# A hybrid layer with linear attention: stores issued by ScalarE, w_out loaded in steps, the sample unit in fourth place

## The chip, the cores and the metric

The kernel runs on one core of a Trainium2 chip. The core has five engines, each with its own row of instructions that it works off in order: TensorE (PE, matrix products; its weight loads are listed as PEld), VectorE (DVE), ScalarE (ACT), GpSimd (POOL) and SyncE (SP), which here does nothing but issue transfers. Transfers between the chip's memory and the core's buffers are issued by an engine and then run beside it. The metric is the time of one execution on the device, in microseconds.

## The reference

One layer of a recurrent decoder is applied to a prompt of 2048 tokens and to a group of samples (8 sequences of 8 tokens, each with states of its own). The width is 1024.

```
h = x @ w_in                               # split into the parts of two head groups
o_gla = rms_norm(gla(q, k, v, log_a, s_gla)) * silu(gate)           # 4 heads
dq, dk, dv = silu(conv(...))               # causal convolution of width 4, then l2 norm of dq, dk
o_gdn = rms_norm(gdn(dq, dk, dv, g, beta, s_gdn)) * silu(gate)      # 4 heads
x = layer_norm(alpha * x + concat(o_gla, o_gdn) @ w_out)
x = layer_norm(alpha * x + (silu(x @ w_gate) * (x @ w_up)) @ w_down)
```

Both attention forms are computed in chunks. In a chunk of GLA the products within the chunk and the product with the state are added, and the state is decayed and raised by k times v. Gated DeltaNet (GDN) solves a triangular system of each chunk first,

```
a_mat = eye + strict_lower(beta * (k k^T) * gamma)
u, w = solve(a_mat, [v * beta, k * beta * exp(gcum)])
delta = u - w @ S
o = (q * exp(gcum)) @ S + ((q k^T) * gamma) @ delta
S = exp(g_last) * S + (k * exp(g_last - gcum))^T @ delta
```

and the next chunk needs its S. Outputs are the layer's result, the new states of prompt and samples, and the last columns of the convolution.

## The kernel before

The 2112 tokens form 17 units: unit 0 holds the 64 sample tokens, units 1 to 16 hold 128 prompt tokens each. Block 0 is the units 0, 1 and 2, and block b the units 1+2b and 2+2b. The stages follow each other in time:

- phase_in, to about 697 us: the projection with w_in, token tiles of 352, weights split into a high and a low part (ScalarE casts the high part at line 185, VectorE subtracts the low part at line 128). The convolution's results cv go to the chip's memory as dq (line 348, 72 stores), the gates as gt and the other parts as qk and v (line 419).
- load_out and phase_gdn, about 697 to 1036 us. load_quad loads w_out in pieces of 128x1024 through two buffers named wraw, scales a piece on VectorE (line 176), casts it on ScalarE (line 177) and subtracts on VectorE. phase_gdn works through groups of units, [0], [1, 2], [3, 4] and so on. rows(b) makes the decay rows of a block, prepare(u) loads q, k and vf of a unit (line 832) and makes its matrix (y at line 846), inversion(group) solves for all units of the group together in seven levels (a product at line 891, a cast P on ScalarE at line 895, products at 898 and 901, copies on VectorE at 904 and 905), advance(u) takes a unit through the state (S at line 940; its result is copied to on at line 263 and stored at 268), and advance_samples does this for unit 0 with the eight states Sh of the sample. While a group advances, the inversion of the next group is done level by level between its products.
- phase_gla, from 1036 us. proj makes gates, q and k of a block and transposes its v (line 527); mix takes the units of the block through the products within the chunk (line 579 and following) and the state; the sample's own states are applied at lines 668 to 696. Between the blocks project(u) does the product with w_out (lines 252 to 254), the layer norm, and stores the transposed result x1T (line 1129) for the next stage. The last nine units are projected after the last block, to about 1450 us.
- The feed-forward part, to the end.

The kernel is written as one program; a scheduler sets the order of each engine's row, by its own estimate of when operands are ready, and by buffers: a tile can be written only when the earlier user of its buffer is done. The two wraw buffers are shared by the pieces of w_out, the sample's states (Sh in GDN, S in GLA) and the x that project adds. keep (lines 256 to 268) copies a result to on, of which there is one buffer, and stores it. All stores are issued by SyncE (ST). A second copy of the GLA stage and what follows stands behind a flag and isn't executed.

## Time and profile before

| what | value |
|---|---|
| time, median of three runs | 2890.68 us (2885.3 to 2898.66) |
| the profiled execution, its own time | 2893.11 us |
| its span | 2891.3 us |
| TensorE busy | 2692.6 us, 93% |
| VectorE busy | 1961.2 us, 68% |
| ScalarE busy | 1229.6 us, 43% |
| GpSimd busy | 1150.5 us, 40% |

The span is the time from the first to the last instruction in the profile; the execution's own time is 1.8 us longer. A busy share is a mean over all stages. Waits are listed with the one that came last. Idle time of an engine counts only where the work that ends the stage waits for it.

### The profile page before, as it was taken

What the parts mean: (1) busy time and instruction counts of PE and PEld (TensorE: products, weight loads), DVE (VectorE), ACT (ScalarE), POOL (GpSimd) and SP (SyncE); (2) the same over time, 40 slices, a digit from 0 to 9 for tenths busy, and PEclk for the clock granted to TensorE, in tenths of its full rate; (3) what the DMA queues carried; (4) which work ended last, traced back from release to release, by engine and by line L of the source; (5) the groups of instructions that cost most, each with busy time, mean ns of one, the idle gap of its engine ahead of it and who ended that gap; (6) DMA issues with size and microseconds to landing.
All of it is one profiled execution on the core that took longest, in us unless ns stands there. A gap on an engine that the chain in (4) does not pass through costs nothing. (4 is left out here: it accounts for less than half of the span.)

```text
span 2891.3 us, 45834 instructions
## 1 busy us (share of the span) xinstructions
PE 2692.6 (93%) x16390; PEld 2451.7 (85%) x16390; DVE 1961.2 (68%) x3185; ACT 1229.6 (43%) x2671; POOL 1150.5 (40%) x1196
## 2 busy tenths in 40 slices
PE   7999999996888868999799999999999999999996
PEld 6998899896777746777589999999999987887885
DVE  7668668665777635776788779877977753646664
ACT  5536536534444323444334445444544432334442
POOL 5343333232543112333586557755555520201111
PEclk9999999998689968999899999999999999999998
DMA  7245235233543033555673326432432334546652
GB/s 252 98 139 190 87 133 168 99 109 116 155 112 85 27 90 113 173 171 162 182 252 115 112 99 204 153 107 99 151 115 102 106 130 139 195 138 232 220 207 91
DMA packets 253156, 406.79 MB, mean 141 GB/s; under 512 B 28488, under 2 KB 211384, under 8 KB 232056
## 3 DMA queue, kind: packets, MB, share of 16 engines
q1 hardware_dynamic: 252488, 403.35, 42.3%
q8 instruction: 131, 2.15, 0.3%
q14 instruction: 105, 0.86, 0.1%
q10 hardware_dynamic: 432, 0.43, 0.0%
HBM read 305.13 MB, written 98.58 MB: 140 GB/s over the span
## 5 line engine op out<-in xcount | busy, mean ns | idle before, releaser
L128 DVE TENSOR_TENSOR wl<-wr,wh 128x512 fp32r<-128x512 f32 x652 | 597.4, 920 | 342.0 <-ACT wh L185 339.3
L229 PE MATMUL p<-xh,wh 128*128 128x352 f32 x2520 | 815.4, 324 | 8.4 <-DVE t L128 4.4
L230 PE MATMUL p<-xl,wh 128*128 128x352 f32 x2520 | 814.6, 323 | 4.1 <-DVE xl L128 4.1
L231 PE MATMUL p<-xh,wl 128*128 128x352 f32 x2520 | 814.4, 323 | 0.7 <-DVE wl L128 0.7
L185 ACT CAST wh<-wr 128x512 fp32r<-128x512 f32 x652 | 402.4, 621 | 581.1 <-PE p L230 283.5
L229 PEld LDWEIGHTS p<-xh,wh 128*128 128x128 f32 x2520 | 474.6, 188 | 10.3 <-ACT wh L185 4.7
L230 PEld LDWEIGHTS p<-xl,wh 128*128 128x128 f32 x2520 | 474.5, 188 | 5.9 <-DVE xl L128 5.9
L231 PEld LDWEIGHTS p<-xh,wl 128*128 128x128 f32 x2520 | 474.0, 188 | 1.0 <-DVE wl L128 1.0
L128 DVE TENSOR_TENSOR t<-t,p 128x352 f32<-128x352 f32 x630 | 318.8, 518 | 202.2 <-PE p L231 200.7
L131 POOL TENSOR_TENSOR wt<-wr 128x512 f32<-128x512 f32 x180 | 243.4, 1352 | 250.0 <-DVE wl L128 222.4
L185 ACT CAST wh<-wt 128x512 fp32r<-128x512 f32 x270 | 167.8, 622 | 316.3 <-PE p L230 271.3
L1051 POOL TENSOR_SCALAR mv<-mv 128x1 f32<-128x1 f32 (+1 forms) x34 | 21.4, 631 | 548.2 <-DVE mv L1050 548.2
L128 DVE TENSOR_TENSOR wl<-wt,wh 128x512 fp32r<-128x512 f32 x270 | 204.9, 759 | 24.2 <-ACT wh L185 20.8
L1237 PE MATMUL p<-wh,hh 128*128 128x512 f32 x528 | 205.4, 389 | 0.0
L1238 PE MATMUL p<-wl,hh 128*128 128x512 f32 x528 | 205.4, 389 | 0.0
L131 POOL TENSOR_TENSOR wt<-wr,wt 128x512 f32<-128x512 f32 x90 | 119.1, 1324 | 212.5 <-DVE wl L128 212.3
L319 PE MATMUL p<-xh,wh 128*128 128x352 f32 x576 | 189.7, 330 | 12.5 <-ACT xh L185 12.5
L1239 PE MATMUL p<-wh,hl 128*128 128x512 f32 x528 | 201.2, 389 | 0.0
L335 DVE SCALAR_TENSOR_TENSOR cv<-hb,cw,cv 128x352 f32<-128x352 f32 (+1 forms) x216 | 151.7, 705 | 58.3 <-ACT cv L333 50.3
L320 PE MATMUL p<-xl,wh 128*128 128x352 f32 x576 | 189.6, 329 | 0.4 <-DVE xl L128 0.4
L321 PE MATMUL p<-xh,wl 128*128 128x352 f32 x576 | 189.8, 330 | 0.0
L131 POOL TENSOR_TENSOR t<-t 128x352 f32<-128x352 f32 x132 | 159.8, 1212 | 53.3 <-ACT t L93 31.2
(278 smaller groups left out, 4790.7 us busy)
## 6 DMA issues: line engine op xcount, KB each, us to landing
wr<-in_w_gu SPq DMA_DIRECT2D x66, 1024.0 KB
wr<-in_w_dn SPq DMA_DIRECT2D x55, 1024.0 KB
wr<-in_w_p SPq DMA_DIRECT2D x42, 1024.0 KB
hid<-t SPq DMA_DIRECT2D x132, 176.0 KB
xr<-in_xT SPq DMA_DIRECT2D x96, 176.0 KB
dq<-cv SPq DMA_DIRECT2D x72, 176.0 KB
xr<-x1T SPq DMA_DIRECT2D x72, 176.0 KB
hr<-hid SPq DMA_DIRECT2D x66, 192.0 KB
```

What stands on the lines that cost most here:

```text
L128: nc.vector.tensor_tensor(out, a, b, op=op)
L131: nc.gpsimd.tensor_tensor(out, a, b, op=op)
L185: nc.scalar.copy(h[:, :N], raw)
L229: nc.tensor.matmul(ps, lhsT=h[:, ks], rhs=x[k][0], start=k == 0, stop=False)
L230: nc.tensor.matmul(ps, lhsT=h[:, ks], rhs=x[k][1], start=False, stop=False)
L231: nc.tensor.matmul(ps, lhsT=l[:, ks], rhs=x[k][0], start=False, stop=k == 3)
L319: nc.tensor.matmul(ps, lhsT=h(k), rhs=x[k][0], start=n == 0, stop=False)
L320: nc.tensor.matmul(ps, lhsT=h(k), rhs=x[k][1], start=False, stop=False)
L321: nc.tensor.matmul(ps, lhsT=l(k), rhs=x[k][0], start=False, stop=n == 7)
L1237: nc.tensor.matmul(p, lhsT=hh[:, ts], rhs=wd[i][0], start=f == 0, stop=False)
L1238: nc.tensor.matmul(p, lhsT=hh[:, ts], rhs=wd[i][1], start=False, stop=False)
L1239: nc.tensor.matmul(p, lhsT=hl[:, ts], rhs=wd[i][0], start=False, stop=f == NF - 1)
```

## The change

1. Stores of results that ScalarE has written are issued by ScalarE: dq (72), gt (48), on (in keep), and x1T (36). The other stores stay on SyncE.
2. load_quad becomes a generator that yields after each piece of w_out. phase_gdn takes one piece after each group, and what is left at the end.
3. The groups of GDN are [1, 2], [3, 4], [5, 6], [0], [7, 8] and so on, and rows(b) is called up to two groups ahead.
4. In GLA the transposes of v move from proj to mix, mix of unit 0 comes behind block 3, and project takes the units in the order 1 to 5, 0, 6 to 16. For the sample the tile at is cleared on GpSimd first.

```diff
-    def load_quad(pool, tag, src, gain):
+    def load_quad(wh, wl, src, gain):
...
             vtt(wl[:, k:k + 2, :], raw, wh[:, k:k + 2, :].bitcast(F32), TT.subtract)
-        return wh, wl
+            yield
...
         if len(dst.shape) == 4:
             for s in range(2):
-                ST.dma_start(out=dst[:, s], in_=on[:C, 2 * s:2 * s + 2])
+                nc.scalar.dma_start(out=dst[:, s], in_=on[:C, 2 * s:2 * s + 2])
         else:
-            ST.dma_start(out=dst, in_=on[:C])
+            nc.scalar.dma_start(out=dst, in_=on[:C])
...
             act(cv, cv, AF.Silu)
             t0 = FT * ib + FN * i
-            ST.dma_start(out=dq_d[f][:, t0:t0 + FN], in_=cv)
+            nc.scalar.dma_start(out=dq_d[f][:, t0:t0 + FN], in_=cv)
...
-                    ST.dma_start(out=to[c + j][:, t0:t0 + FN], in_=t)
+                    (nc.scalar if to is gt_d else ST).dma_start(out=to[c + j][:, t0:t0 + FN], in_=t)
...
         for b in range(NBLK):
-            mix(b, proj(b))
+            r = proj(b)
+            if b == 0:
+                r0 = r
+            mix([u for u in blocks[b][2] if u], r)
+            if b == 3:
+                mix([0], r0)
             yield
...
-        groups = [[0]] + [[u, u + 1] for u in range(1, NU, 2)]
+        groups = [[u, u + 1] for u in range(1, NU, 2)]
+        groups.insert(3, [0])
+        blk = [us[0] // 2 for us in groups]
...
         rows(0)
         start(0)
+        rows(1)
         for _ in inversion(groups[0]):
             pass
         start(1)
         for n, us in enumerate(groups):
+            if n + 2 < len(groups) and blk[n + 2] > 1:
+                rows(blk[n + 2])
...
             for _ in steps:
                 pass
+            next(more, None)
             start(n + 2)
+        for _ in more:
+            pass
...
+        order = [1, 2, 3, 4, 5, 0] + list(range(6, NU))
...
-                project(b)
+                project(order[b])
```

VectorE's row at the start of the GDN stage, before: wraw is a piece of w_out, o1l the low part of its second half, y and at belong to a unit (64x4x64 is the sample, 128x512 a prompt unit), and wr, lr, grs and rr are decay rows.

```order
L773 SCALAR_TENSOR_TENSOR grs_7833<-misc_61,lr_8030 8x256
L128 TENSOR_TENSOR o1l_7796<-wraw_7797,o1h_7795 128x1024
L775 SCALAR_TENSOR_TENSOR rr_8032<-nr_8031,grs_7833 4x256
L176 TENSOR_SCALAR wraw_7802<-wraw_7802,gain_7771 128x1024
L764 TENSOR_SCALAR wr_8626<-wr_8626,gsc_7826 8x256
L846 SCALAR_TENSOR_TENSOR y_7934<-g_7929,gb_7917 64x4x64
L128 TENSOR_TENSOR at_7948<-g_7943,gb_7917 64x4x64
L176 TENSOR_SCALAR wraw_7807<-wraw_7807,gain_7771 128x1024
```

The same engine at its first y in the changed kernel:

```order
L764 TENSOR_SCALAR wr_7983<-wr_7983,gsc_7786 8x256
L128 TENSOR_TENSOR o0l_7774<-wraw_9544,o0h_7773 128x1024
L426 TENSOR_SCALAR wr_7983<-wr_7983 8x256
L128 TENSOR_TENSOR lr_7984<-wr_7983,ls_7990 8x256
L767 TENSOR_SCALAR lr_7984<-lr_7984,gsc_7786 8x256
L773 SCALAR_TENSOR_TENSOR grs_7793<-misc_61,lr_7984 8x256
L775 SCALAR_TENSOR_TENSOR rr_7986<-nr_7985,grs_7793 4x256
L764 TENSOR_SCALAR wr_8428<-wr_8428,gsc_7786 8x256
L846 SCALAR_TENSOR_TENSOR y_7894<-g_7889,gb_7877 128x512
L128 TENSOR_TENSOR at_7908<-g_7903,gb_7877 128x512
```

The first y is now that of unit 1; of the pieces of w_out only the first three stand ahead of it (the third one's subtraction is the second row here), and the other five stand some 300 rows further down.

ScalarE's row where units 3 and 4 are advanced, before and then changed: P is the cast in the inversion, on the copy of a unit's result, on1 its place in the chip's memory.

```order
L895 CAST P1_7838<-inv_8860 128x64x4
L93 ACTIVATE c_rq_176<-c_r_177,lnq_7831 128x4
L93 ACTIVATE ckh_10222<-ckh_10222 128x4
L263 COPY on_9110<-po_9101 128x512
L93 ACTIVATE eR_10220<-R_10218 128x4x129
L93 ACTIVATE nr_10688<-nr_10688,epsl_69 8x256
L895 CAST P2_7839<-inv_8877 128x32x8
```

```order
L840 COPY vt_9577<-g_9572 128x512
L895 CAST P0_7797<-inv_8966 128x128x2
L262 COPY on_9100<-po_9091 128x512
L895 CAST P1_7798<-inv_8983 128x128x2
L267 DMA on1_3_91<-on_9100 128x512
L93 ACTIVATE eR_10221<-R_10219 128x4x129
L895 CAST P2_7799<-inv_9000 128x64x4
```

In the changed kernel the store (line 267) stands one row behind its copy, or two, and the casts of the next level stand behind the store.

TensorE's row at the sample's place in GLA, before (527 transposes v, 579 and 634 begin a unit, 668, 682 and 690 are the sample's own, 944 and 945 the end of GDN):

```order
L944 MATMUL po<-S,qe 128x128
L945 MATMUL po<-de,at 128x128
L944 MATMUL po<-S,qe 128x128
L945 MATMUL po<-de,at 128x128
L944 MATMUL po<-S,qe 128x128
L945 MATMUL po<-de,at 128x128
L527 MATMUL g<-ident,vf 64x128 x4
L527 MATMUL g<-ident,vf 128x128 x8
L579 MATMUL g<-qz_12297,kn 64x2x64 x2
L634 MATMUL g<-ident,ek 64x128 x2
L668 MATMUL px<-v,at_12303 64x128 x2
L682 MATMUL px<-S_12399,qm 64x128 x4
```

The same place in the changed kernel, where these lines have the numbers 531, 574, 629, 663, 677 and 685, and 647 is the last product of unit 8:

```order
L643 MATMUL g<-S,qz_12298 128x128
L647 MATMUL g<-v,kz 128x128 x4
L531 MATMUL g<-ident,vf 64x128 x4
L574 MATMUL g<-qz_12297,kn 64x2x64 x2
L629 MATMUL g<-ident,ek 64x128 x2
L663 MATMUL px<-v,at_12303 64x128 x2
L677 MATMUL px<-S_13278,qm 64x128 x4
L685 MATMUL g<-v,khm 64x128 x2
L677 MATMUL px<-S_13278,qm 64x128 x4
L685 MATMUL g<-v,khm 64x128 x2
```

The sample's products now stand behind those of unit 8; no product with w_out stands between them.

## Rows read from the trace of the kernel before

**Rows 1.** The page of the profile: the span, TensorE's busy time, and the row of the forty slices (72.3 us each) for TensorE's busy share, in tenths.
```profile
span 2891.3 us, 45834 instructions
...
PE 2692.6 (93%) x16390; PEld 2451.7 (85%) x16390; DVE 1961.2 (68%) x3185; ACT 1229.6 (43%) x2671; POOL 1150.5 (40%) x1196
...
PE   7999999996888868999799999999999999999996
```

**Rows 2.** Busy time by stretches of 20 us, the stretch, its length, then busy us and number of instructions of PE, PEld, DVE, ACT and POOL, the granted clock (1.00 is full), the DMA engines' share and GB/s. The first row lies in the projections, the next five in the GDN stage, the last three at the start of the GLA stage.
```profile
480.00:500.00 20.00, 18.45 (x101) 15.07 (x101) 17.71 (x27) 12.66 (x30) 13.38 (x17) 1.00 0.42 138
700.00:720.00 20.00, 4.67 (x25) 3.15 (x25) 14.26 (x31) 8.95 (x20) 6.87 (x12) 0.50 0.81 215
720.00:740.00 20.00, 10.27 (x50) 9.12 (x51) 18.25 (x27) 14.68 (x39) 15.47 (x24) 0.50 0.57 154
740.00:760.00 20.00, 20.00 (x126) 18.11 (x126) 10.38 (x18) 8.12 (x23) 11.52 (x12) 0.59 0.77 209
...
780.00:800.00 20.00, 16.38 (x147) 14.76 (x146) 17.65 (x36) 6.32 (x21) 7.68 (x10) 0.84 0.70 191
900.00:920.00 20.00, 15.52 (x205) 14.22 (x206) 14.04 (x33) 7.62 (x18) 6.11 (x7) 0.91 0.17 45
1040.00:1060.00 20.00, 9.00 (x46) 6.75 (x46) 7.12 (x24) 5.79 (x15) 5.33 (x12) 0.52 0.76 201
1060.00:1080.00 20.00, 14.95 (x89) 10.69 (x84) 4.29 (x16) 2.79 (x13) 2.67 (x11) 0.50 0.15 44
1080.00:1100.00 20.00, 18.00 (x71) 9.59 (x72) 6.32 (x17) 1.98 (x8) 2.66 (x5) 0.70 0.17 44
```

**Rows 3.** VectorE's timeline in the GDN stage (start, duration, both in us): the cast with which the inversion of a pair begins (line 128, DT from inv), and the update of S (line 940) of the first unit of the pairs (1, 2), (3, 4) and (5, 6), and of unit 16, the last.
```profile
817.62 1.28 DVE L128 TENSOR_TENSOR DT<-inv,half 128x512 f16<-128x512 f32 x2
...
819.81 1.12 DVE L940 SCALAR_TENSOR_TENSOR S<-S,eGl,seq 128x128 f32<-128x128 f32 x4 [0.21 <-PE seq L938]
...
854.39 1.12 DVE L940 SCALAR_TENSOR_TENSOR S<-S,eGl,seq 128x128 f32<-128x128 f32 x4 [0.21 <-PE seq L938]
...
884.81 1.12 DVE L940 SCALAR_TENSOR_TENSOR S<-S,eGl,seq 128x128 f32<-128x128 f32 x4 [0.21 <-PE seq L938]
...
1035.28 1.12 DVE L940 SCALAR_TENSOR_TENSOR S<-S,eGl,seq 128x128 f32<-128x128 f32 x4 [3.14 <-PE seq L938]
```

**Rows 4.** VectorE's timeline at the start of the GDN stage: y (line 846) of the sample (64 rows), of unit 1 and of unit 2 (128 rows each), and the cast that begins the inversion of the pair (1, 2).
```profile
721.36 0.42 DVE L846 SCALAR_TENSOR_TENSOR y<-g,gb 64x256 f32<-64x256 f32 x1
...
736.42 0.69 DVE L846 SCALAR_TENSOR_TENSOR y<-g,gb 128x512 f32<-128x512 f32 x1
...
744.41 0.69 DVE L846 SCALAR_TENSOR_TENSOR y<-g,gb 128x512 f32<-128x512 f32 x1 [0.18 <-PE g L844]
...
765.42 1.27 DVE L128 TENSOR_TENSOR DT<-inv,half 128x512 f16<-128x512 f32 x2
```

**Rows 5.** ScalarE's timeline there: gb, the operand of y, of unit 1.
```profile
723.45 1.28 ACT L93 ACTIVATE gb<-R,c_nb 128x128 f32<-128x128 f32 x4
```

**Rows 6.** Groups of instructions of the GDN stage (690 to 1040 us; line, engine, operation, tiles, shapes and count, then busy us and mean ns of one, then the idle time before them and what ended it): TensorE's four large groups for the sample, whose lines no other unit uses.
```profile
L993 PE MATMUL seq<-de,khm 64*128 64x128 f32 x64 | 13.1, 369 | 0.5 <-DVE Sh L128 0.5
...
L966 PE MATMUL seq<-kq,Sh 128*128 128x16 f32 x64 | 12.6, 344 | 2.6 <-DMA Sh<-in_state_gdn 2.6
...
L982 PE MATMUL po<-ident,fm 128*64 128x128 f32 x8 | 2.8, 448 | 0.0
L983 PE MATMUL po<-de,at 64*64 64x128 f32 x8 | 2.7, 445 | 0.0
```

**Rows 7.** The same view: VectorE's work on the pieces of w_out, eight in all (the scale, and the low part of the second four).
```profile
L176 DVE TENSOR_SCALAR wraw<-wraw,gain 128x1024 f32<-128x1024 f32 x8 | 9.2, 1156 | 5.5 <-DMA wraw<-in_w_out 4.6 <-DMA gain<-in_norm_g 0.9
...
L128 DVE TENSOR_TENSOR o1l<-wraw,o1h 128x1024 fp32r<-128x1024 f32 x4 | 5.1, 1273 | 0.0
```

**Rows 8.** ScalarE's queue at the start of the program: one of the transfers that it issues (start, duration of the issue).
```profile
1.16 0.45 ACTq L304 DMA_DIRECT2D hist<-in_conv  x1
```

**Rows 9.** Waits: who waited at which line for whom, us in all, times, longest. First ScalarE and then TensorE up to 700 us, then TensorE in the GDN stage.
```profile
ACT wh L185 <- PE p L230: 163.7, 146, 1.4
...
PE p L319 <- ACT xh L185: 12.5, 2, 8.3
...
PE inv L898 <- ACT P L895: 24.5, 48, 0.8
```

**Rows 10.** Waits of SyncE's DMA queue over the whole span, the same columns: the stores of on and of x1T.
```profile
SPq L268 <- ACT on L263: 156.9, 14, 22.3
...
SPq L1129 <- ACT x1T L1125: 37.3, 17, 5.2
```

**Rows 11.** TensorE's timeline from the end of the GDN stage: the last product of GDN, the transposes of v (with the wait ahead of them in brackets), the sample's first product, and the first transposes for w_out after the sample's run.
```profile
1036.42 0.39 PE L945 MATMUL po<-de,at 128*128 128x128 f32 x2
1047.74 2.02 PE L527 MATMUL g<-ident,vf 128*64 128x128 f32 x8 [10.93 <-DMA vf<-v]
...
1054.04 1.11 PE L579 MATMUL g<-qz,kn 128*64 128x128 f32 x4
...
1081.67 0.69 PE L1102 MATMUL pt<-ident,on 64*128 64x64 f32 x4 [1.74 <-DVE on L128]
```

**Rows 12.** SyncE's queue at the same place (start and duration of the issues).
```profile
1037.49 0.32 SPq L268 DMA_DIRECT2D on<-on  x1
...
1041.35 1.32 SPq L524 DMA_DIRECT2D vf<-v  x2
```

More of the change, by code (lines that the diff above doesn't have):

```diff
@@ L167, in hybrid_layer @@
     psg = ctx.enter_context(tc.tile_pool(name="psg", bufs=2, space=PSUM))
-    def load_quad(pool, tag, src, gain):
-        wh, wl = (pool.tile([128, 8, 512], F32R, name=tag + p, tag=tag + p, bufs=1) for p in "hl")
+    def load_quad(wh, wl, src, gain):
         v = src.rearrange("(k p) c -> p k c", p=128)
@@ L520, in proj, with mix @@
                 per_unit(nm, t, ts)
+            return r
+        def mix(us, r):
             for u in us:
                 u0, C = units[u]
+                smp = u == 0
+                q, k, la = (r[n, u] for n in ("q", "k", "la"))
                 vf = p1.tile([128, 4, 128], F32, name="vf", bufs=2)
@@ L527, in proj @@
                     nc.tensor.transpose(pt[:C, h, :], vf[:, h, :C], ident)
-                t = p1.tile([128, 4, 128], F32, name="v", tag="v", bufs=3)
-                nc.scalar.copy(t[:C], pt[:C])
-                r["v", u] = t
-            return r
-        def mix(b, r):
-            c0, T, us = blocks[b]
-            for u in us:
-                u0, C = units[u]
-                smp = u == 0
-                cs = slice(u0 - c0, u0 - c0 + C)
-                q, k, la = (r[n, u] for n in ("q", "k", "la"))
-                v = r["v", u]
+                v = p1.tile([128, 4, 128], F32, name="v", tag="v", bufs=3)
+                nc.scalar.copy(v[:C], pt[:C])
                 bt = p1.tile([128, 2 * C], F32, name="bt", tag="bt")
@@ L569, in mix @@
                     count["at"] += 1
+                    if smp:
+                        nc.gpsimd.memset(at, 0.0)
                     nc.gpsimd.tensor_copy(lows[:, :, 0:8] if smp else lows[:, :, 7 + u:8 + u],
@@ L714, in phase_gla, with phase_gdn @@
         yield
-    def phase_gdn(stack):
+    def phase_gdn(stack, more):
         pe = stack.enter_context(tc.tile_pool(reuse_waits=RW, name="pe", bufs=2, side="right"))
@@ L1013, in inversion @@
             yield
-        groups = [[0]] + [[u, u + 1] for u in range(1, NU, 2)]
+        groups = [[u, u + 1] for u in range(1, NU, 2)]
+        groups.insert(3, [0])
+        blk = [us[0] // 2 for us in groups]
         def start(n):
             if n < len(groups):
-                if n:
-                    rows(n) if n < NBLK else None
                 for u in groups[n]:
@@ L1064, in load_out, with steps @@
         nc.sync.dma_start(out=gain, in_=I["norm_g"])
-        return [load_quad(po, f"o{i}", I["w_out"][:, 512 * i:512 * i + 512], gain) for i in range(2)]
+        wo = [[po.tile([128, 8, 512], F32R, name=f"o{i}{p}") for p in "hl"] for i in range(2)]
+        def steps():
+            for i in range(2):
+                yield from load_quad(*wo[i], I["w_out"][:, 512 * i:512 * i + 512], gain)
+        return wo, steps()
     def phase_out(stack, wo, gla, ffn):
@@ L1128, in project @@
                     if a < e:
-                        ST.dma_start(out=x1T_d[fb][4 * i:4 * i + 4, :, a - FT * fb:e - FT * fb].rearrange("k p t -> p k t"),
+                        nc.scalar.dma_start(out=x1T_d[fb][4 * i:4 * i + 4, :, a - FT * fb:e - FT * fb].rearrange("k p t -> p k t"),
                                      in_=t[:, :, a - u0:e - u0])
+        order = [1, 2, 3, 4, 5, 0] + list(range(6, NU))
         with ExitStack() as g:
@@ L1135, in phase_out @@
                 next(parts, None)
-                project(b)
+                project(order[b])
             next(parts, None)
         next(ffn)
-        for u in range(NBLK, NU):
+        for u in order[NBLK:]:
             project(u)
@@ L1261, in hybrid_layer @@
         out = ExitStack()
-        ahead["wo"] = load_out(out)
+        ahead["wo"], more = load_out(out)
         with ExitStack() as stack:
-            phase_gdn(stack)
+            phase_gdn(stack, more)
         finish(rest, out, phase_gla)
@@ L1271, in hybrid_layer @@
         out = ExitStack()
-        ahead["wo"] = load_out(out)
+        ahead["wo"], more = load_out(out)
+        for _ in more:
+            pass
         finish(rest, out)
```

## Prediction

> **What bounds the kernel now.** I read the page's shares and its forty slices first, then the busy time of each engine by stretches, and then, only where TensorE is not full, the timelines and the waits. TensorE is busy for 2692.6 of 2891.3 us [rows 1]. The slices show where the other 199 us are: in the row of PE the slices 10 to 16 (72.3 us each, so 650 to 1156 us: the GDN stage and the start of the GLA stage) stand at 6 to 8, and slice 20 (1373 to 1445 us) at 7 [rows 1]. In the projections TensorE is all but full: 18.45 of 20 us at clock 1.00 [rows 2]. So the change can win only between about 690 and 1450 us; in front of that it can only disturb. In 700 to 720 us TensorE works 4.67 of 20 us and VectorE 14.26; in 720 to 740 us 10.27 and 18.25, at a granted clock of 0.50, the lower of its two levels (1.2 GHz of 2.4) [rows 2]. From 760 us on the stage runs at 15 to 17 of 20. There the chain is the prompt state: S is updated unit after unit, in pairs that lie 34.6 and 30.4 us apart (from 819.81 to 854.39 to 884.81; unit 16, the last, comes at 1035.28) [rows 3]. What comes ahead of 819.81 is the lead-in, and the change is about that.
>
> **The change, part by part.**
>
> *Sample fourth in GDN.* Before, unit 0 (the sample) goes first and alone, and the pair (1, 2) stands behind it. I split the lead-in from y of unit 1 to the first S. (a) y of unit 1 is computed at 736.42, yet its last operand, gb, is there at 723.45 + 1.28 = 724.73 [rows 4, 5]; what holds it is the sample's work in TensorE's row and the w_out pieces on VectorE. Without them y comes at about 724.7: 11.7 us. (b) y of unit 2 follows 8.0 us later, which I keep. From it to the pair's first D transposed (765.42) there are 21.0 us, in which the sample's own inversion runs; now that cast stands a few rows behind y, some 2 us: 19.0 us. (c) From that cast to the first S: 54.4 us before, with the sample's advance mixed in. The next pair, which has only the previous pair's advance beside it, takes 854.39 - 817.62 = 36.8 us [rows 3]. I take that: 17.6 us. At most the sample's whole 31.2 us of TensorE would go (below), at least nothing. Sum 48.3 us, bounds 31 and 62. The step to the second pair, 34.6, should become the later 30.4: another -4 (0 to -4).
>
> Then the sample must still be paid for in its new place. Its four large TensorE groups sum to 12.6 + 13.1 + 2.8 + 2.7 = 31.2 us [rows 6], taken at clocks of 0.59 to 0.84 (say 0.70) [rows 2]; at the 0.91 of 900 to 920 us this is 31.2 x 0.70 / 0.91 = 24 us. In that stretch TensorE idles 4.5 of 20 us, about 7 us in a 30 us step; the new order sets the sample's matmuls between the inversion levels of units 7 and 8, so part of that idle time takes them up. I count 4 us hidden: +20. Ends: 17 (all of the 7 us hidden) and 31.2 (nothing hidden, no better clock).
>
> *w_out in steps.* Three of the eight pieces stay in the lead-in (the sample's states, prefetched into the same two buffers, hold up the rest), five go behind the sample. A piece is a scale of 1.16 us and a subtraction of 1.27 us on VectorE [rows 7], so 5 x 2.4 = 12 us leave 700 to 740 us (that gain is inside (a)) and land where VectorE is busy 14.04 of 20 us [rows 2]. With a third of the time free there I charge a third: +4 (0 to 12).
>
> *Stores issued by ScalarE.* 72 dq, 48 gt, about 51 on and 36 x1T pass from SP to ScalarE. An issue on ScalarE's queue takes 0.45 us [rows 8]. ScalarE goes through its row in order, so each store also waits there until its result is written, and what stands behind waits too. In the projections the 120 stores cost 120 x 0.45 = 54 us plus a wait for the activation just ahead of them, for which no row stands; I put it at up to as much again. ScalarE works 12.66 of 20 us there [rows 2], and it spends 163.7 us waiting for buffers that TensorE frees, so its casts are ahead of TensorE; TensorE's longest sum of waits for ScalarE before 700 us is 12.5 us, in two waits [rows 9]. This lead covers the issues; without it each would cost its 0.45 us. I charge +3 (-3 to +15). In GDN 17 issues, 17 x 0.45 = 7.7 us, stand directly behind the copy of on, and the next cast of the inversion (P) queues behind them: TensorE waits for those casts 48 times already, 24.5 us in all [rows 9]. +3 (0 to 8). x1T: SP has been waiting 37.3 us there [rows 10], now it is free for the loads behind: -2 (-5 to +5).
>
> What SP gains in the GDN stage: it stood 156.9 us at the store of on, with loads queued behind [rows 10]. Yet TensorE waited for a DMA in that stage only once, 2.6 us [rows 6]. The loads are early enough: 0 (-3 to 0). The Trainium skill, DMA: Bandwidth & Descriptors, section "Issuing engines are not separate DMA queues", says that another issuing engine saves no more than the issuing sequencer's time, since the transfers share the same DMA engines. By that rule the stores are worth nothing or their cost of +4 as above, by SP's 156.9 us read as lost time up to -157; the one wait of 2.6 us is on the rule's side.
>
> *Sample after block 3 in GLA.* Before, TensorE waits 10.93 us for v from 1036.8 us on, then does the sample alone from 1054.04 to 1081.67 at a clock of 0.50, and then the first W_out product [rows 2, 11]. SP issues v nearly 4 us behind on, after the norm's two rows and q, qs, k, ks [rows 12]; in the new order only on has left that row (ScalarE issues it), so the wait stays. Units 1 and 2 then start at the low clock, and the sample runs later, still with no product of W_out between its matmuls, since the next x of the projection waits for the buffer that the sample's state holds. Its 27.6 us contain about 20 us of TensorE at 0.50, which would be 11 at 0.9, -9; units 1 and 2, which before ran after the clock had come up to 0.70 [rows 2], lose some 3. I take -6 (-15 to +10; the upper end is the 11 us wait once more, in the new place). In the Trainium skill, TensorE: Matmul & The Clock Gate, section "HAM oscillation — how this bites in real kernels", waits for DMAs are what lowers the clock again and again; if the sample's own waits did that at its new place too, this term would be 0 and the sum -24. The row of 1060 to 1080 us, 14.95 busy at 0.50, speaks neither for nor against.
>
> *Feed-forward.* The order of every engine there is unchanged: 0.
>
> Sum: -48.3 - 4 + 20 + 4 + 3 + 3 - 2 - 6 = -30.3 us. On the profiled execution, 2893.1 us (the span and 1.8 us around it), that gives 2862.8; the median shown is 2.4 us below that execution, so 2860 us.
>
> **The rivals.**
> - *The lead-in goes and little comes back.* (c) wins 31.2 instead of 17.6 us, the sample costs 17, VectorE and ScalarE hide theirs, GLA gains 12: -61.9 - 4 + 17 - 12 = -61, 2830 us. For it: TensorE idles 4.5 of 20 us in the middle of the stage. Against: the chain of S is a chain of four engines, and idle time in it is waiting that other work lengthens.
> - *What the sample saves at the front it costs in the middle.* 31.2 for the sample, 12 for w_out and 8 for on, against -48.3 and -4, all else 0: -1, 2890 us, no change. For it: the sample's states, w_out and the projection's x share two buffers, so a wait for one is handed on. Against: the clock is at 0.5 to 0.6 where the sample stands now.
> - *ScalarE becomes the engine that is waited for.* One store that waits for its activation holds up the casts of the next weights (wh, xh). If half of the 120 in the projections cost TensorE 0.45 us twice over, that is +54 in place of their +3, with the other terms +21: 2912 us, slower. It decides as soon as ScalarE's lead is used up: at 12.66 of 20 us and four to six stores in a 20 us stretch (3.6 to 5.4 us) it stands at 16.3 to 18.1 of 20, which is close. Against: the 163.7 us of lead. That is also the case in which the stores do nothing for SP and only harm.
>
> **How the numbers follow.** The forecast's chance is 0.52, its own range 2844 to 2880; the deep gain has 0.23, no change 0.17, slower by ScalarE 0.08. About 0.5% (14.5 us: below 2876 or above 2905) is what a measurement of this kernel can tell from no change. Faster: 0.48 of the forecast's 0.52 and the whole deep case, 0.71. Within: 0.04 of the forecast and 0.15 of the third case, 0.19. Slower: 0.08 and 0.02 from the upper end of the third case, 0.10. The range from 2818 to 2897 holds the forecast, 0.17 of the deep case and 0.12 of the third, 0.8.
>
> **What would show it.** Right: the first S of the prompt near 771 us of a stage that starts at 697, pairs 30 us apart, one step some 20 us longer in the group with the sample, the last S near 1011; the first 700 us within 5 us of before; TensorE's wait for v of about 10 us still there at the end of GDN; the sample's matmuls in GLA at a clock well above 0.50. Wrong: TensorE waits named after ScalarE's casts in the projections (the third rival); a first S later than 790 us; a step with the sample that is 35 us longer than its neighbours; or GLA stretches that grow because the sample's state waits for the projection's buffer.

## The result and the profile after

The changed kernel is slower: 2931.03 us (median of four runs, 2919.52 to 2935.23) against 2894.27 us, ratio 1.0125, 95% interval 1.0084 to 1.0166. The forecast was 2860 us, faster, with a range up to 2897. The profiled execution of the changed kernel took 2919.52 us, 26.4 us more than that of the kernel before; it is the fastest of the four, the medians lie 36.8 us apart, and what follows accounts for the profiled pair. The page of the changed kernel, to be read beside [rows 1]; the last line is ScalarE's queue (packets, MB, share of the 16 engines):

```profile
span 2917.7 us, 45672 instructions
...
PE 2697.6 (92%) x16390; PEld 2455.0 (84%) x16390; DVE 1958.4 (67%) x3185; ACT 1230.9 (42%) x2671; POOL 1144.8 (39%) x1197
...
PE   7999999997688869798789999999999999999996
...
q10 hardware_dynamic: 48096, 39.38, 4.1%
```

TensorE's busy time is nearly the same. The dips begin at slice 10 as before. Slice 10 has risen from 6 to 7, slice 11 has fallen from 8 to 6, slices 17 and 19 have fallen to 7 and 8, and slice 21 has become a dip.

The updates of S divide the execution into stages that can be measured one by one. VectorE's updates of S in the changed kernel (the first unit of each pair, and the last unit), beside [rows 3]:

```profile
777.64 1.12 DVE L940 SCALAR_TENSOR_TENSOR S<-S,eGl,seq 128x128 f32<-128x128 f32 x4 [0.21 <-PE seq L938]
...
812.79 1.12 DVE L940 SCALAR_TENSOR_TENSOR S<-S,eGl,seq 128x128 f32<-128x128 f32 x4 [1.01 <-PE seq L938]
...
847.90 1.12 DVE L940 SCALAR_TENSOR_TENSOR S<-S,eGl,seq 128x128 f32<-128x128 f32 x4 [0.81 <-PE seq L938]
...
923.94 1.11 DVE L940 SCALAR_TENSOR_TENSOR S<-S,eGl,seq 128x128 f32<-128x128 f32 x4
...
964.17 1.12 DVE L940 SCALAR_TENSOR_TENSOR S<-S,eGl,seq 128x128 f32<-128x128 f32 x4 [0.44 <-PE seq L938]
...
1052.00 1.12 DVE L940 SCALAR_TENSOR_TENSOR S<-S,eGl,seq 128x128 f32<-128x128 f32 x4 [3.09 <-PE seq L938]
```

The first S comes at 777.64, 42.2 us earlier than before. The pairs then lie 35.2 and 35.1 us apart, the step with the sample takes 923.94 - 847.90 = 76.0 us, the step behind it 40.2 us, and the last S stands at 1052.00, where it stood at 1035.28. So 42.2 us are won in front and 58.9 us are lost behind: 16.7 us later. From the last S to the first product of the feed-forward part it takes 425.9 us (to 1477.93), before 413.2 us (to 1448.46): another 12.7 us. What comes behind is 3.0 us shorter. 16.7 + 12.7 - 3.0 = 26.4.

The stretch with the sample, from S to S, and below it an ordinary step of the kernel before (columns as in [rows 2]):

```profile
847.90:923.94 76.04, 70.06 (x582) 61.40 (x580) 45.78 (x91) 19.86 (x49) 22.90 (x32) 0.73 0.46 128
...
854.39:884.81 30.42, 26.36 (x324) 24.45 (x323) 23.70 (x58) 14.95 (x39) 12.41 (x18) 0.89 0.33 88
```

TensorE is busy 70 of 76 us, at a mean granted clock of 0.73. This is no wait; it is more work, and at low speed. The step has 258 more entries of TensorE (the number in brackets) than the ordinary one: 144 are the sample's four groups [rows 6], 52 are other products of the sample (its inversion and lines 973 and 977), and 62 belong to the prompt units beside it. The timeline shows where the clock goes:

```profile
858.12 2.85 PE L966 MATMUL seq<-kq,Sh 128*128 128x16 f32 x24
...
862.31 2.06 PE L855 MATMUL g<-q,k 128*128 128x128 f32 x8
...
885.40 2.07 PE L993 MATMUL seq<-de,khm 64*128 64x128 f32 x8
...
916.97 1.16 PE L855 MATMUL g<-q,k 128*128 128x128 f32 x8
```

Behind the sample's first products (line 966, of 16 columns) the eight ordinary products of line 855 take 2.06 us. Eight of the same line at 916.97 take 1.16 us. In between the clock has mostly been at its lower level, and the products of the sample's state update (line 993) took 2.07 us for eight. The last eight of that line, at 910.90, took 1.16 us again. In the stretch from 880 to 900 us TensorE was busy 19.02 of 20 us, and the clock was 0.50 from end to end (the last row; the first two are the stage's start, beside [rows 2]):

```profile
700.00:720.00 20.00, 5.74 (x27) 4.94 (x28) 11.35 (x28) 11.56 (x27) 7.41 (x12) 0.63 0.68 184
720.00:740.00 20.00, 10.78 (x58) 8.83 (x58) 15.62 (x25) 11.08 (x31) 15.23 (x24) 0.67 0.42 108
880.00:900.00 20.00, 19.02 (x102) 14.99 (x100) 9.21 (x18) 3.45 (x8) 0.60 (x1) 0.50 0.34 90
```

Behind the GDN stage the longest waits of TensorE are these (beside [rows 9], same columns):

```profile
PE pw L251 <- ACT oh L1119: 34.2, 13, 7.3
PE g L531 <- DVE qz L552: 10.1, 1, 10.1
PE g L574 <- DVE qz L552: 9.6, 3, 7.7
```

The wait of the w_out products (pw) for oh, their left operand as ScalarE casts it, was 16.5 us before.

### The profile page after: what moved, and what is told of

The parts are those of the page before. It is cut to its first block, busy times and chain, and to the rows that moved or that the text cites. A ratio compares the mean times of both kernels' runs of the same rounds, so it can differ in the third digit from the quotient of the medians.

```text
span 2917.7 us, 45672 instructions
## 1 busy us (share of the span) xinstructions
PE 2697.6 (92%) x16390; PEld 2455.0 (84%) x16390; DVE 1958.4 (67%) x3185; ACT 1230.9 (42%) x2671; POOL 1144.8 (39%) x1197
## 5 line engine op out<-in xcount | busy, mean ns | idle before, releaser
L128 DVE TENSOR_TENSOR wl<-wr,wh 128x512 fp32r<-128x512 f32 x652 | 589.6, 908 | 343.9 <-ACT wh L184 334.8
```

The source lines that it names most:

```text
L128: nc.vector.tensor_tensor(out, a, b, op=op)
```

## The experiments

Each ratio is to the kernel before, run on the same chip. The table holds for each kernel what the prediction's steps are about: the first S, the length of the step with the sample (an ordinary step is 30 us), the last S, the time from the last S to the first product of the feed-forward part (stage), the time from the last S to the end of the span (rest, which includes the stage), and TensorE's wait for oh behind the last S, all in us. All but the ratios are read from one profile per kernel. x1_wide, x2_few, y1_fill and y2_fill3 further down were run once each and have no ratio.

| kernel | first S | step with sample | last S | stage | rest | TensorE waits for oh | ratio and interval |
|---|---|---|---|---|---|---|---|
| before | 819.8 | - | 1035.3 | 413.2 | 1856.0 | 16.5 | 1 |
| changed | 777.6 | 76.0 | 1052.0 | 425.9 | 1865.7 | 34.2 | 1.0125 (1.0084-1.0166) |
| e1_stores | 824.8 | - | 1043.0 | 431.7 | 1871.1 | 39.0 | 1.0067 (1.0037-1.0096) |
| e2_gdn | 786.9 | 68.7 | 1051.8 | 408.4 | 1850.2 | 18.6 | 1.0027 (1.0007-1.0048) |
| e3_gla | 822.5 | - | 1039.1 | 427.4 | 1867.8 | 41.8 | 1.0061 (1.0039-1.0083) |
| e4_wout | 804.3 | - | 1028.2 | 429.3 | 1871.8 | 33.7 | 1.0037 (1.0019-1.0055) |
| g3_early_oh | 782.8 | 83.1 | 1061.9 | 407.6 | 1861.7 | none | 1.0087 (1.0061-1.0114) |
| g4_wout_early_oh | 818.5 | - | 1043.0 | 416.8 | 1863.1 | none | 1.0009 (0.9992-1.0027) |
| h1_gt | 823.7 | - | 1039.1 | 423.9 | 1868.6 | 35.4 | 1.0037 (1.0019-1.0054) |
| h2_dq | 825.1 | - | 1045.1 | 411.3 | 1854.5 | 15.7 | 1.0020 (1.0006-1.0034) |
| i1_wout_two_first | 808.6 | - | 1029.5 | 404.4 | 1846.5 | 15.1 | 0.9946 (0.9926-0.9965) |
| i2_wout_x1T | 804.5 | - | 1026.1 | 395.7 | 1837.5 | 10.6 | 0.9895 (0.9878-0.9913) |
| j1_i1_gdn | 778.1 | 83.9 | 1060.8 | 406.4 | 1851.4 | 18.1 | 1.0051 (1.0030-1.0072) |

Single profiles of kernels that are alike in front of the GDN stage differ by some 4 us: the last product of the projections ends between 694.5 and 698.4 us in the twelve kernels that leave the stores of dq and gt on SyncE. So differences of that size in the absolute times of the first and last S say nothing. In the four kernels that move the stores of dq it ends between 698.1 and 701.8 us, 3.8 us later in the mean.

### One part at a time

e1_stores is item 1 of the change alone, e2_gdn the order of the GDN groups alone, e3_gla item 4 alone, e4_wout item 2 alone, each put into the kernel before.

> The kernel before with only the stores of dq, gt, on and x1T issued by ScalarE. Theory A (the stores on ScalarE do the harm: each sits in ScalarE's row in front of the casts of the inversion and of the projection's normalised result): ratio 1.006 to 1.012, pairs of the GDN stage longer by about 5 us each, TensorE's waits for the cast P up by 9 us or more, and the wait of the w_out products for oh up from 16.5 to above 30 us. Theory B (the sample's place does the harm, the stores do next to nothing): ratio 0.998 to 1.003, stage lengths within 4 us of before, S of unit 1 near 819.

> The kernel before with only the order of the GDN groups changed (sample fourth, rows called earlier); all of w_out at the front and all stores on SyncE. Theory B (the sample's narrow products pull TensorE's clock down in the middle of the stage and hold up the inversion of units 7 and 8): S of unit 1 near 785 to 795 (w_out in front costs up to 12 us of the 42 won), pairs of 30 us as before, but a step of 70 us or more around the sample with a granted clock near 0.50, last S near 1045, ratio 1.002 to 1.006. Theory A: the step around the sample is near 50 us, last S near 1020 and ratio 0.993 to 0.997.

> The kernel before with only the GLA side changed (transposes of v in mix, mix of unit 0 behind block 3, projection in the order 1 to 5, 0, 6 to 16). Theory B: from the last S of GDN to the first product of the feed-forward part 420 to 425 us instead of 413, ratio 1.002 to 1.005, the loss around the sample. Theory A: this length is within 4 us of before and the ratio 0.998 to 1.002.

> The kernel before with only w_out taken in steps, one piece after each group. If the pieces were what held up the first y, S of unit 1 comes 5 to 12 us earlier and the ratio is 0.996 to 0.999; if they were hidden behind the sample, the ratio is 0.999 to 1.002 and S of unit 1 within 3 us of 819.8. By neither theory does it lengthen a pair by more than 2 us.

Each of the four is slower by itself, and the four losses (0.67, 0.27, 0.61 and 0.37%) sum to 1.9%, more than the whole change costs. So something in them is counted several times. The table shows what: the stage behind GDN is 427 to 432 us in e1, e3 and e4, though they have no edit in common, and 408 us in e2. The first expectation of e1 was right in its ratio and in the wait for oh and wrong in its reason: the pairs of GDN are hardly longer than before (their seven steps sum to 211.1 us, before 209.1), and TensorE's waits for the cast P rose by 3.4 us and not by 9, so the 17 stores of on go with about 2 us there. For e2 theory B had the ratio and the first S right; its pairs are longer than expected (36.7 and 34.1 us), and its step with the sample is 68.7 us at a mean clock of 0.78 and not of 0.50. e3 is worse than either theory said, in its stage and in its ratio. e4 fits neither of its theories: S of unit 1 comes 15.5 us earlier, the step behind it is 39.5 us where 34.6 stood, and the kernel is slower. It wins 7.1 us at the last S and loses 16 us in a stage in which w_out is no longer loaded at all.

What e1, e3, e4 and the changed kernel share is an order. In the kernel before, other work of the GLA stage stands on TensorE between the transposes (pt) of a unit's result and its first product with w_out (pw):

```profile
1257.31 1.03 PE L1102 MATMUL pt<-ident,on 128*128 128x128 f32 x8
1258.18 0.39 PE L646 MATMUL g<-v,at 128*128 128x128 f32 x2
...
1259.97 1.06 PE L652 MATMUL g<-v,kz 128*128 128x128 f32 x8
1263.01 0.50 PE L252 MATMUL pw<-o0h,oh 128*128 128x512 f32 x1 [1.98 <-ACT oh L1107]
```

In e1_stores pw stands a few products behind pt:

```profile
1250.66 1.03 PE L1102 MATMUL pt<-ident,on 128*128 128x128 f32 x8
1251.53 1.03 PE L579 MATMUL g<-qz,kn 128*128 128x256 f32 x4
1252.40 0.38 PE L634 MATMUL g<-ident,ek 128*128 128x128 f32 x2
1255.65 0.70 PE L252 MATMUL pw<-o0h,oh 128*128 128x512 f32 x1 [2.87 <-ACT oh L1107]
...
1257.43 0.63 PE L646 MATMUL g<-v,at 128*128 128x128 f32 x2
```

TensorE takes its row in order. While the operand passes through VectorE and ScalarE, the first kernel does 2.7 us of products of line 646 to 652 and then waits 1.98 us; the second one waits 2.87 us with the same products behind, and the products of line 646 after the wait take 0.63 us a pair instead of 0.39. Counted over the units in the middle of the stage, 8 or 24 entries of TensorE stand between pt and pw in the kernel before, in e2, h2, i1, i2 and j1, and 2 to 6 in e1, e3, e4, h1 and in most units of the changed kernel. (These are entries of the trace, of which one product can leave two; the expectations below count otherwise.) No line of the kernel asks for this. The scheduler sets it, by its estimate of times, and a change hundreds of microseconds earlier tips it over.

### The order behind GDN

> The changed kernel, with the operands of each product with w_out (normalising, transposes, oh and ol) given a higher priority in the scheduler, so that other work of TensorE stands between the transposes and the product. Theory O (the GLA and W_out stage is longer because the products with w_out now stand two to four instructions behind their own transposes, before eight to twelve): TensorE's wait for oh falls from 34 to below 15 us, the stage from 425.9 to 408 to 415 us, ratio 1.006 to 1.009. Rival (the stage is longer by the sample's place and by ScalarE's stores): stage within 5 us of 425.9, ratio near 1.0125.

> e4_wout (only w_out in steps) with the same higher priority for the operands of the products with w_out. Theory O: the stage from 429.3 down to 405 to 413 us, while the GDN stage keeps its 7 us (last S near 1028), ratio 0.993 to 0.998: faster than both kernels. Rival: stage above 424 us, ratio 1.002 or more.

```diff
+            with tc.high_priority(1000):      # g3_early_oh; 300 in g4_wout_early_oh
                 for g in range(2):
                     on = pi.tile([128, 512], F32, name="on", bufs=2)
...
```

This is a clumsy tool. The wait for oh is gone, and the stage is shorter, 407.6 for 425.9 us and 416.8 for 429.3. But the priority moves other things too: the first product of the feed-forward part now stands ahead of the last transposes of x, for which TensorE waits 15.3 us in g3, and the rest from the last S to the end is only 4.0 and 8.7 us shorter. In g4 the first S was back at 818.5, and its stage, last S and ratio all missed what was expected. The ratios are lower than without the priority, though their intervals overlap, and neither kernel is faster than the one before. On the size these two decide nothing.

The cleaner test needs two kernels with the same work in the stage and another order only. Moving the 48 stores of gt tips the order over, moving the 72 stores of dq doesn't, and all of them lie before 700 us.

```diff
-                    ST.dma_start(out=to[c + j][:, t0:t0 + FN], in_=t)
+                    (nc.scalar if to is gt_d else ST).dma_start(out=to[c + j][:, t0:t0 + FN], in_=t)     # h1_gt
...
-            ST.dma_start(out=dq_d[f][:, t0:t0 + FN], in_=cv)
+            nc.scalar.dma_start(out=dq_d[f][:, t0:t0 + FN], in_=cv)                                      # h2_dq
```

> The kernel before with only the 48 stores of gt issued by ScalarE. They all lie in the projections, before 700 us; in the stages behind them the same instructions run on the same engines as before. What differs there is the scheduler's order: the products with w_out now stand two to four of TensorE's instructions behind their own transposes, before eight to twelve. Theory O (this order is what lengthens the GLA and W_out stage): from the last S to the first product of the feed-forward part 427 to 432 us, before 413, TensorE's wait for oh 34 us or more, ratio 1.004 to 1.008. Rival (ScalarE's own issues lengthen it): stage 411 to 416 us, ratio 0.999 to 1.003.

> The kernel before with only the 72 stores of dq issued by ScalarE; the order of TensorE in the later stages is that of before. Theory O: stage of GLA and W_out 411 to 416 us, the projections within 3 us, ratio 0.998 to 1.002. Rival (stores on ScalarE in the projections delay the casts of the weights): the projections 5 us longer or more, ratio 1.003 or more.

TensorE's longest waits behind the GDN stage, first h1_gt:

```profile
PE pw L252 <- ACT oh L1107: 35.4, 17, 7.3
PE g L527 <- DMA vf<-v: 13.7, 2, 10.4
```

then h2_dq:

```profile
PE pw L252 <- ACT oh L1107: 15.7, 11, 6.2
PE g L527 <- DMA vf<-v: 13.6, 2, 10.3
```

The second row is alike. The stage is 423.9 against 411.3 us (expected 427 to 432 and 411 to 416), the rest 14.1 us longer. The two stages (columns as in [rows 2]), first h1_gt:

```profile
1039.06:1462.97 423.91, 347.14 (x1822) 280.37 (x1820) 261.17 (x490) 159.54 (x537) 166.71 (x234) 0.88 0.53 161
```

then h2_dq:

```profile
1045.14:1456.49 411.35, 345.94 (x1822) 279.17 (x1820) 261.54 (x490) 159.65 (x537) 148.53 (x226) 0.89 0.53 158
```

TensorE's work and clock are nearly the same; almost all of the difference is idle time, 76.8 against 65.4 us. The ratios, 1.0037 (a little below what theory O expected) and 1.0020, lie closer, since h2 has a loss of its own ahead of this stage: its interval puts the stores of dq at 2 to 10 us of 2892, and its projections end later than was expected of it, as the rival had it.

The distance between pt and pw is a mark and not the whole of it: y1_fill (below) has 2 to 6 entries there and waits 29.8 us for oh, and its stage is 411.7 us all the same. In the middle of the stage, from the end of the sixth unit's products with w_out to that of the fourteenth's, h2 takes 158.2 us, h1 163.6 and y1 163.2. So the short distance goes with some 1.3 us more for each pair of units there, 5 of the 12.5 us. The other 7 lie with the first and the last units, where y1 is quicker than h1; what in the order makes them was not found. GpSimd's row differs as well: it is busy 164 to 168 us in this stage in all the kernels whose stage is 424 us or longer, and 144 to 153 in the kernel before, e2, h2, i1, i2, j1 and y1. Whether that is a cause or follows from the longer stage was not tested.

Two forms of e4_wout with the longer distance:

```diff
+        next(more)              # i1_wout_two_first: two pieces of w_out ahead of the first group
+        next(more)
         rows(0)
         start(0)
...
-                        ST.dma_start(out=x1T_d[fb][4 * i:4 * i + 4, :, ...
+                        nc.scalar.dma_start(out=x1T_d[fb][4 * i:4 * i + 4, :, ...      # i2_wout_x1T
```

> e4_wout with two pieces of w_out taken ahead of the first group and the other six one after each group; in this form the products with w_out keep the eight to twelve instructions behind their transposes. Theory O: the 7 us that e4_wout wins in the GDN stage stay (last S near 1029), and the stage behind it is back to 411 to 416 us: ratio 0.995 to 0.999, faster than both kernels. Rival: that stage is 425 us or more, ratio 1.003.

> e4_wout with the stores of x1T issued by ScalarE as well; again the products with w_out stand eight to twelve instructions behind their transposes. Theory O: last S near 1029, stage behind it 408 to 416 us, ratio 0.994 to 0.999. Rival (the stores of x1T on ScalarE delay the copies oh): that stage is 425 us or more and the wait for oh above 30 us, ratio 1.003.

Both are faster than the kernel before and than the changed one, i2_wout_x1T by 1% (2862.91 against 2892.19 us), and both stages, 404.4 and 395.7 us, are shorter than was expected. i2_wout_x1T keeps the sample first, takes w_out in steps and lets ScalarE issue only x1T. Against e4_wout one line differs, and the rest is 34 us shorter:

```profile
PE g L526 <- DMA vf<-v: 13.8, 2, 10.6
PE px L1131 <- DVE xt L1060: 11.2, 1, 11.2
PE pw L251 <- ACT oh L1115: 10.6, 9, 6.2
```

The wait for oh is down to 10.6 us. How much of the 34 us is the order and how much the stores of x1T was not taken apart; i1_wout_two_first, with x1T on SyncE, has 25 us of it. Between the sixth and the fourteenth unit, where both have the same distance, i2 takes 150.1 us and i1 157.7, so the stores of x1T on ScalarE do no harm and may help; that was not tested by itself.

### The step with the sample

> e2_gdn with the 64 products of the sample with its states (Sh stationary) moving 128 columns each in place of 16; the weights loaded and the number of products stay the same. The results of the sample are not the reference's. Theory C (the clock: products that move few columns pull TensorE down to 0.50 in the middle of the stage): the granted clock of the step with the sample rises from 0.78 to 0.9 or more, and the step of 68.7 us gets no longer, perhaps 5 us shorter, though each product moves eight times the columns. Theory W (the work: TensorE is full in this step, and each product costs by its columns): clock near 0.78, step 5 to 12 us longer.

> e2_gdn with 16 products of 64 columns in place of 64 of 16 columns for the first product of the sample with its states (one state of four is used, so three quarters of this work is left out and the sample's results are not the reference's). Theory C: the clock of the step rises to 0.9 or more and the step falls from 68.7 us by more than 15 us, more than the 8 us that the 48 products take. Theory W: the step falls by 6 to 9 us, the clock stays within 0.05 of 0.78. If neither more than 4 us, TensorE is not what the step waits for.

```diff
-                    nc.tensor.matmul(pf[:, h, s], lhsT=Sh[:, s, :], rhs=kq[:, h, :, 8 * s:8 * s + 8],
+                    nc.tensor.matmul(pw4[:, s % 4], lhsT=Sh[:, s, :], rhs=kq[:, h],          # x1_wide
...
-                for s in range(NSEQ):
+                for s in range(0, NSEQ, 4):                                                  # x2_few: 64 columns each
```

Both theories missed, in both runs. The step is 72.8 us with the wide products and 72.5 us with three quarters of them left out; e2_gdn has 68.7. The mean clock was 0.77 and 0.72. In x1_wide the clock stays at 1.00 from 870 to 880 us, where e2_gdn has 0.60, but then it is at 0.50 from 890 to 910 us; in x2_few from 890 to 910 us as well. So the first products of the sample are not what decides; the clock falls at one place or another of the step. x2_few's text has a third outcome, a change of no more than 4 us either way, by which TensorE is not what the step waits for. The step is 3.8 us longer, so that reading was open; it takes the clock as given, which fell from 0.78 to 0.72 here.

What holds in all of these kernels is the length of the step times its mean granted clock: 76.0 x 0.73 = 55.5 in the changed kernel, 68.7 x 0.78 = 53.6 in e2_gdn, 56.1 in x1_wide, 55.7 in g3_early_oh, 54.5 in j1_i1_gdn, and 52.2 in x2_few, which leaves work out. Steps from 68.7 to 83.9 us long thus come out, by this estimate, as one and the same step of 54 to 56 us at full clock. So far this is a reading of five profiles; the next experiment puts it to the test. It gives TensorE more to do:

```diff
+            for _ in range(1 if w.get("fill") else 0):          # 3 in y2_fill3; units 7 and 8
+                nc.tensor.matmul(pP[:, 0:3, :], lhsT=i16, rhs=half[:, 0:3, :], start=True, stop=True)
...
                     pS = pmt("seq")
+                    for _ in range(1):                          # 3 in y2_fill3
+                        nc.tensor.matmul(pS[:, 0:3, :], lhsT=i16, rhs=half[:, 0:3, :], start=True, stop=True)
```

> e2_gdn with products added that change no result: in the step with the sample, one product of 384 columns (of constants) ahead of each level of the inversion of units 7 and 8, ahead of each group of four products of the sample's state update, and fewer columns ahead of the first products. Their outputs are overwritten by the products behind them. About 25 of them, 4 to 8 us more work for TensorE. Theory C (the half clock in this step is what makes it 15 to 27 us too long): the granted clock of the step rises from 0.78 to 0.88 or more and the step gets shorter than 68.7 us, to 60 to 66. Theory W (TensorE's work alone): the clock stays and the step grows by 4 to 8 us.

> The same with three of the added products at each place, 12 to 25 us more work for TensorE. Theory C: clock 0.95 or more, step 62 to 72 us. Theory W: clock as in e2_gdn, step 80 to 95 us.

> i1_wout_two_first with the sample fourth in the GDN stage as well. The products with w_out keep their eight to twelve instructions behind the transposes. If the sample's new place costs by itself (a step of 65 to 80 us against 30, of which the lead-in gives back some 20 to 25): last S near 1045 against 1029.5, stage behind it 404 to 409 us, ratio 0.998 to 1.003, 10 to 20 us behind i1_wout_two_first. If it cost only in company with the other parts: within 4 us of i1_wout_two_first.

The step from S to S in e2_gdn:

```profile
857.63:926.36 68.73, 63.90 (x556) 57.13 (x555) 40.75 (x88) 19.05 (x48) 23.62 (x32) 0.78 0.53 145
```

in y1_fill:

```profile
852.10:919.40 67.30, 62.49 (x580) 54.57 (x578) 39.69 (x88) 19.15 (x48) 23.70 (x32) 0.87 0.53 148
```

in y2_fill3:

```profile
852.00:924.90 72.90, 68.06 (x625) 56.21 (x624) 41.43 (x87) 18.70 (x48) 24.12 (x32) 0.91 0.49 137
```

With some 24 more products on TensorE the clock is 0.87 in place of 0.78 and the step 67.3 us in place of 68.7. Length times clock is 58.5, so at full clock the step has become 5 us longer, and it takes no more time. With three times the filling it is 0.91 and 73.0 us (66.4 at full clock). At e2_gdn's clock of 0.78 these two would have lasted, by estimate, 58.5 / 0.78 = 75 and 66.4 / 0.78 = 85 us. Theory W expected an unchanged clock and a step of 73 to 77 us in y1 and of 80 to 95 us in y2; neither came. Theory C has the direction of the clock; its sizes were a little too good in both runs (0.88 and 60 to 66 us, 0.95 and 62 to 72 us). So the step's length does hang on the clock. In y1 the filling pays for itself, within what single profiles can tell; in y2 it doesn't.

In j1_i1_gdn, the same step at the lowest clock of all:

```profile
849.60:933.50 83.90, 78.18 (x583) 69.50 (x581) 46.05 (x91) 19.99 (x49) 23.87 (x32) 0.65 0.42 116
```

j1_i1_gdn differs from i1_wout_two_first by the sample's place alone, and both have the good order behind. The last S is 31.2 us later and the ratio 1.0051 instead of 0.9946. The sample's place costs by itself. Expected were 10 to 20 us, and a last S near 1045 where it came at 1060.8.

## Why the prediction was wrong

- **The lead-in** (48.3 us forecast, 42.2 measured): right in the sum, and partly by luck, since its four parts were off by 4 to 8 us each, two up and two down. Of them, y of unit 1 came at 720.44, 16.0 us earlier (11.7 forecast). y of unit 2 follows 16.2 us later, not 8.0. From it to the second unit's cast 8.9 us remain (2 forecast), and from there to S 32.0 us (36.8 forecast):

```profile
720.44 0.69 DVE L846 SCALAR_TENSOR_TENSOR y<-g,gb 128x512 f32<-128x512 f32 x1
...
736.67 0.68 DVE L846 SCALAR_TENSOR_TENSOR y<-g,gb 128x512 f32<-128x512 f32 x1
...
745.59 0.69 DVE L128 TENSOR_TENSOR DT<-inv,half 128x512 f16<-128x512 f32 x1 [0.87 <-PE inv L879]
```

- **The next step, 30.4 instead of 34.6**: wrong, it stayed at 35.2, and the second one rose from 30.4 to 35.1. Together 9 us. In e2_gdn, with no other part of the change, they are 36.7 and 34.1, so it is the new group order that does it (rows and prepare of the sample are made in these steps).
- **The sample in its new place** (+20 forecast, 76.0 - 30.4 = +45.6 measured): the step that failed. The prediction took the clock of the stretch of 900 to 920 us, 0.91, for granted in a step with other work, counted 4 us as hidden, and priced the sample's four large groups alone: the sample's inversion is taken out of the front as a gain under (b) and charged nowhere. At 0.91 the step would have been, by estimate, 55.5 / 0.91 = 61 us, 10.6 us above forecast: the 4 us that were not hidden, and 6.6 us for products that were not priced (the 52 others of the sample, and the 62 of the units beside it). The other 15 us are the clock, 0.73. The rival "what the sample saves at the front it costs in the middle" is nearest to what came, but its price, 31.2 us for the sample, was too small as well; I had put the low clock down as a property of the place in front. It comes with the sample's step, and a row of the prediction could have told: from 740 to 760 us [rows 2], where 50 of the 64 entries of line 966 lie, TensorE is busy 20.00 of 20 us at a clock of 0.59.
- **w_out in steps** (+4): 10.6 us in the step behind the sample, 40.2 instead of 29.6, of which e2_gdn has 3.4 with w_out in front. The other 7 lie within the stated 0 to 12. Alone, e4_wout gives 7.1 us at the last S; the sum has that gain under (a), together with the sample's.
- **Stores on ScalarE** (+3, +3, -2): in the GDN stage about right (+2). In front of it the profiles with dq's stores moved end 3.8 us later in the mean, so the +3 was about right; h2's interval, 2 to 10 us for dq alone, allows more. An issue took 0.33 us in the median for dq and gt, where 0.45 was taken. The rival of a ScalarE that is waited for in the projections did not come: TensorE's waits for its casts before 700 us are 13.0 us in two waits, before 12.5. SyncE's 156.9 us of waiting at the store of on brought nothing, as forecast: in e1_stores, which moves these stores too, the seven steps are no shorter, 211.1 us against 209.1. The Trainium skill, DMA: Bandwidth & Descriptors, section "Issuing engines are not separate DMA queues", says that issuing from another engine saves no more than the issuing sequencer's time; those two numbers agree with it.
- **The sample's place in GLA** (-6): its run did get shorter, 1187.32 to 1208.46 = 21.1 us for 27.6. But the start of the stage keeps a wait (10.14 us) of the forecast size, though the profile names VectorE's qz for it and not the transfer of v, and there is a new one of 7.71 us ahead of unit 7, where no product with w_out stands in TensorE's row until 1212.10:

```profile
1063.67 0.66 PE L531 MATMUL g<-ident,vf 128*128 128x128 f32 x2 [10.14 <-DVE qz L552]
...
1172.76 2.04 PE L574 MATMUL g<-qz,kn 128*128 128x256 f32 x4 [7.71 <-DVE qz L552]
...
1187.32 0.62 PE L574 MATMUL g<-qz,kn 128*64 128x128 f32 x4 [0.35 <-DVE S L651]
...
1208.46 0.68 PE L1114 MATMUL pt<-ident,on 64*128 64x64 f32 x4 [2.50 <-DVE on L128]
```

- **"The order of every engine there is unchanged: 0"** was said of the feed-forward part and held (-3.0). What was not looked at is the order of the products with w_out between 1050 and 1480 us. It is in no term of the sum and no rival: e1, e3, e4 and h1 each lose 11 to 19 us in that stage, and what they share is this order. That an order alone can do it is shown by h1 against h2; which part of the order does it is shown for 5 of their 12.5 us. How the changed kernel's 12.7 us divide between this order and the new wait in GLA was not taken apart.

## What to carry to other kernels

When a scheduler sets the order, a change in one stage can reorder another one far behind it; compare the order of the engine that bounds the kernel over the whole program, above all how far each product stands behind the instructions that make its operand, and judge a part of a change only where that order is the same. Small products don't fill the gaps of a full engine for free: where a step moves to a place in which TensorE is busy, count all of its products, those too whose absence was booked as a gain, and don't price them at the clock of the new place. And split a change that loses: of the four parts here, w_out in steps together with the stores of x1T was worth 1% of the time, and the sample's new place in GDN costs as much (j1_i1_gdn against i1_wout_two_first).

## What had not been expected of the hardware

The granted clock stood at 0.50, the lower level, while TensorE was busy 19.02 of 20 us (880 to 900 us of the changed kernel). Over the whole of 862 to 910 us it was 0.57 in the mean, with TensorE busy 44.25 of 48 us, and it went up to 1.00 and down again in between. It fell first at 862 us, after TensorE had worked without a gap since 848 us at a clock of 1.00. The Trainium skill, TensorE: Matmul & The Clock Gate, section "HAM oscillation — how this bites in real kernels", speaks of waits for DMAs as what lowers the clock; here TensorE waited for no DMA from 848 to 910 us. What lowered it here stays open. And added products that compute nothing raised it, from 0.78 to 0.87 and 0.91 in the mean of the step.
